# A written instruction order for the first tiles and weight units of a hybrid encoder step

## The chip, the cores and the metric

The kernel runs on one core of one Trainium2 chip. The metric is the device time of one execution in microseconds (us): before the change 1288.83 us, the median of three runs from 1287.74 to 1289.24.

## The reference

Two layers act on 640 token rows (512 of a prompt, 8 groups of 16 of a sample), each 1024 channels wide. Layer 0 is a chunked gMLP, layer 1 an attention with a forgetting bias. The change touches only the start of layer 0:

```python
hp = rms_norm(xp, norm_pre[i])                     # x * rsqrt(mean(x*x) + 1e-6) * g
proj = h @ w_in                                    # (rows, 1024) @ (1024, 6144)
uv = jax.nn.gelu(proj[..., :2 * E])                # E = 2048: u, then v; z is the last third
v = layer_norm(uv[..., E:], ln_g, ln_b)            # v = the second third of proj
```

What follows (the mask over chunks, the product with the gate, the attention, the output projections, the per-layer embedding) is the same code on both sides.

## The kernel before, in words

The 640 rows are five tiles of 128 (t = 0 to 4; four of the prompt, one of the sample). The third of the projection that gives v is computed first, in four panels p of 512 columns. For one panel the product runs over the 1024 channels in eight blocks of 128 (k = 0 to 7); five accumulators, one per tile, stand in five banks of the accumulation memory (pb, eight banks).

Products are made precise by splitting: each operand becomes a high part, rounded to a short format by ScalarE (ACT, line 289), and a low part, the rest, by VectorE (DVE, line 290). One product is then three matmuls on TensorE (PE): high by high, high by low, low by high (lines 272, 273, 274, in the function `mm3`). So one panel has 5 x 8 x 3 = 120 matmuls of 128x512.

Weights come in units of 512 KB, two channel blocks each (unit u has blocks 2u and 2u+1), through three buffers (RAW) into five places for split units (W). SyncE (SP) issues their loads from one list; a load into a RAW buffer waits until the split of the unit before in that buffer is done. `prefetch` splits units as far ahead as W has room, `weights(1)` hands out the next one.

A tile of x (two loads of 256 KB) is brought into the product's form in this chain: squares and their sum (the left half on ACT, line 423, the right on DVE, 424); the two sums added (427); mean and eps (301); the power -1/2 on GpSimd (POOL, 303); x scaled by it and by the gain, half by half (DVE, 431; the gain is broadcast over partitions by a matmul with ones into banks 3 and 4, line 410, and read from there); each half transposed in four 128x128 blocks on PE (317) into one of the banks 5, 6, 7; and split into high and low (289, 290) into A, whose first 4 channel blocks come from the left half.

Before the products there are matmuls on zeros: three at the start (401) and four (N_FILL) between tile 0's two transposed halves (417).

A scheduler that works with its own model of times puts the instructions of each engine in an order. The program text sets it only where it says so: `tc.issue_after(x)` (in the helper `queued`) keeps an instruction behind x on its engine. Before the change this is used at the start for the filling matmuls, for tile 1's squares and for the first weight split.

Of the kernel before, what the change touches and what calls it, by code (L numbers as in the profile page):

```python
# [19 lines left out]
AF = mybir.ActivationFunctionType  # L20
# [37 lines left out]
def hybrid_trunk(tc, x_prompt, x_sample, ck, cv, clf, p_prompt, p_sample, norm_pre, norm_post,  # L58
# [34 lines left out]
    def f(ap):  # L93
        return ap.bitcast(F32)
# [201 lines left out]
    def rstd_of(ss, eps, mean=False, keep=False):  # L296
        t = small()
        if mean:
            nc.vector.tensor_scalar(out=t, in0=ss, scalar1=eps, scalar2=None, op0=ALU.add)
        else:  # L300
            nc.vector.tensor_scalar(out=t, in0=ss, scalar1=1.0 / D, scalar2=eps, op0=ALU.mult, op1=ALU.add)  # L301
        q = small(keep=keep)
        behind["pool"] = nc.gpsimd.tensor_tensor(out=q, in0=t, in1=mhalf, op=ALU.pow)  # L303
        return q
# [79 lines left out]
    def r2(o, n, p=P):  # L384
        return R2[:p, o:o + n]
# [5 lines left out]
    warm = r2(8320, 512)  # L391
    nc.gpsimd.memset(grow, 0.0)
    nc.vector.memset(warm, 0.0)
    nc.vector.memset(ones, 1.0)
# [4 lines left out]

    for i in range(N_WARM):  # L400
        nc.tensor.matmul(PB[7][:, :256], warm[:, :P], warm[:, 256:], start=True, stop=True)
    fetch(1)
    for t in range(1, NT):
        for h in range(2):
            x_dma(nc.sync, t, h)
        fetch(t // 2 + 1)
    dma(CST[:, P:], consts[:, P:])
    gb = PB[3], PB[4]
    for h in range(2):
        nc.tensor.matmul(gb[h], ones, grow[:, h * 512:(h + 1) * 512], start=True, stop=True)  # L410

    def first_tile(c, hi, bv):
        if c == 0:
            behind["act"] = hi
            for i in range(N_FILL):
                with queued("pe"):
                    behind["pe"] = nc.tensor.matmul(PB[2][:, :256], warm[:, :P], warm[:, 256:], start=True, stop=True)

    for t in range(NT):
        x, xn = r2(t * D, D), r2(5120 + (t % 2) * D, D)  # L420
        ss = [small(), small()]
        with queued(*["act", "dve"] * (t == 1)):
            nc.scalar.activation(out=xn[:, :512], in_=x[:, :512], func=AF.Square, accum_out=ss[0])
            nc.vector.scalar_tensor_tensor(out=xn[:, 512:], in0=x[:, 512:], scalar=1.0, in1=x[:, 512:], op0=ALU.mult, op1=ALU.mult,
                                           accum_out=ss[1])
        sq = small()
        nc.vector.tensor_tensor(out=sq, in0=ss[0], in1=ss[1], op=ALU.add)
        rs = rstd_of(sq, RMS_EPS)
        for h in range(2):
            hs = slice(h * 512, (h + 1) * 512)  # L430
            behind["dve"] = nc.vector.scalar_tensor_tensor(out=xn[:, hs], in0=x[:, hs], scalar=rs, in1=gb[h], op0=ALU.mult, op1=ALU.mult)
        transposed_split(xn, lambda c: h_hi[:, 4 * c:4 * c + 4, t * P:(t + 1) * P],
                         lambda c: h_lo[:, 4 * c:4 * c + 4, t * P:(t + 1) * P], (5, 6, 7), first_tile if t == 0 else None)
        with queued(*["dve"] * (t == 0)):
            prefetch(t + 1)


    o_X, o_ln, o_sum, o_th = 14208, 15232, 16256, 17216
    HT = TOK // 2
# [828 lines left out]
```

## Time and profile before

| | |
|---|---|
| median of three runs | 1288.83 us |
| the profiled execution | 1288.87 us, of it span 1287.1 us |
| PE busy | 1271.9 us, 99% of the span |
| DVE, ACT, POOL busy | 962.9, 592.3, 356.6 us |
| granted PE clock over the span | 0.999 |
| first product of panel 0 starts | 11.18 us after the span's start |

The times of the profile are counted from the start of the span. PE is busy nearly throughout; matmuls overlap, so the length of one row is more than what it costs when others follow it, and the step from one start to the next is the price. The prediction shows the rows it uses.

### The profile page before, as it was taken

To read this page: it belongs to the slowest core of one execution; us is meant where nothing else is said; L and a number is where in the kernel's file an instruction comes from. 1 tells how busy PE (TensorE), PEld (TensorE's weight loads), DVE (VectorE), ACT (ScalarE), POOL (GpSimd) and SP (SyncE) were. 2 spreads that over 40 slices of the span, in tenths; PEclk is the share of its full clock that TensorE was granted. 3 is DMA by queue.
4 is the path that set the end of the run, shared out by engine and by line. 5 is a ranking of instruction groups with operands and counts; after the bars stand their busy time and mean duration, and the time that the engine had idled before them with its cause. 6 is when DMAs were issued, how large, how long until landed. Compare 5 with 4: busy or idle time off the path is not lost.

```text
span 1287.1 us, 21134 instructions
## 1 busy us (share of the span) xinstructions
PE 1271.9 (99%) x7881; PEld 1140.2 (89%) x7881; DVE 962.9 (75%) x1805; ACT 592.3 (46%) x1071; POOL 356.6 (28%) x328
## 2 busy tenths in 40 slices
PE   8999999999999999998999999999999999999998
PEld 6888999999988888887899999998999999788887
DVE  6744999999943364797987898989898988645643
ACT  4423554544545253563445454545444444545331
POOL 1012445454000010245344444444344430000100
PEclk9999999999999999999999999999999999999999
DMA  6432343323324212647787867677788748732211
GB/s 232 131 99 82 100 126 108 111 79 103 117 88 162 84 42 95 149 99 155 159 171 164 189 158 168 145 173 163 146 158 190 177 104 257 257 127 82 66 66 49
DMA packets 275264, 171.52 MB, mean 133 GB/s; under 512 B 188761, under 2 KB 238473, under 8 KB 275162
## 3 DMA queue, kind: packets, MB, share of 16 engines
q1 hardware_dynamic: 261170, 127.80, 36.2%
q0 software_dynamic: 10080, 36.89, 14.0%
q10 hardware_dynamic: 3912, 5.50, 1.3%
q8 instruction: 62, 1.02, 0.3%
q14 instruction: 40, 0.33, 0.1%
HBM read 148.55 MB, written 21.59 MB: 132 GB/s over the span
## 4 chain that ended last, share of the span: by engine, by line
PE 94%; DVE 3%; DMA 2%; issue 0%; ACT 0%; SPq 0%; POOL 0%; DVEq 0%; ACTq 0%; POOLq 0%
PE pb L272 27%; PE pb L273 27%; PE pb L274 27%; PE pb L1055 3%; PE pb L1132 1%; PE pb L1048 1%; PE pb L317 1%; PE pb L1105 1%; PE pb L621 1%; DVE W L290 1%; PE pb L920 1%; DMA R<-in_cache_fox_k 1%; PE pb L933 1%; DMA RAW<-in_gmlp_w_in 1%; PE pb L1129 1%; DMA r2a_t<-in_x_prompt 0%
## 5 line engine op out<-in xcount | busy, mean ns | idle before, releaser
L272 PE MATMUL pb<-A,W 128*128 128x320 f32 (+1 forms) x752 | 240.8, 320 | 2.9 <-DVE R L600 2.5
L273 PE MATMUL pb<-A,W 128*128 128x320 f32 (+1 forms) x752 | 233.7, 311 | 0.0
L274 PE MATMUL pb<-A,W 128*128 128x320 f32 (+1 forms) x752 | 233.2, 310 | 0.0
L290 DVE TENSOR_TENSOR W<-RAW,W 128x1024 fp32r<-128x1024 f32 (+1 forms) x126 | 152.9, 1214 | 74.7 <-ACT W L289 72.5
L272 PE MATMUL pb<-W,A 128*128 128x512 f32 x520 | 204.2, 394 | 0.6 <-ACT A L289 0.5
L273 PE MATMUL pb<-W,A 128*128 128x512 f32 x520 | 203.2, 391 | 0.6 <-DVE W L290 0.5
L274 PE MATMUL pb<-W,A 128*128 128x512 f32 x520 | 202.5, 392 | 0.0
L289 ACT ACTIVATE W<-RAW 128x1024 fp32r<-128x1024 f32 (+1 forms) x126 | 120.0, 953 | 95.2 <-PE pb L274 47.7
L272 PEld LDWEIGHTS pb<-A,W 128*128 128x128 f32 x752 | 141.7, 188 | 4.0 <-DVE R L600 2.7
L273 PEld LDWEIGHTS pb<-A,W 128*128 128x128 f32 x752 | 141.6, 188 | 0.6 <-issue 0.2
L274 PEld LDWEIGHTS pb<-A,W 128*128 128x128 f32 x752 | 141.2, 188 | 0.0
L303 POOL TENSOR_TENSOR SML<-SML 128x1 f32<-128x1 f32 x25 | 19.2, 771 | 372.6 <-DVE SML L301 367.9
L272 PE MATMUL pb<-tbf,W 128*128 128x320 f32 x360 | 119.0, 330 | 0.0
L273 PEld LDWEIGHTS pb<-W,A 128*128 128x128 f32 x520 | 97.7, 188 | 20.8 <-DVE W L290 1.4
L272 PEld LDWEIGHTS pb<-W,A 128*128 128x128 f32 x520 | 97.7, 188 | 20.5 <-ACT A L289 1.1
L274 PEld LDWEIGHTS pb<-W,A 128*128 128x128 f32 x520 | 97.5, 188 | 20.6 <-DVE A L290 0.5
L274 PE MATMUL pb<-tbf,W 128*128 128x320 f32 x360 | 111.4, 309 | 0.0
L273 PE MATMUL pb<-tbf,W 128*128 128x320 f32 x360 | 111.2, 309 | 0.0
L211 POOL TENSOR_TENSOR sff<-RAW 128x512 f32<-128x512 f32 x46 | 59.2, 1289 | 172.6 <-DVE W L290 111.3
L589 DVE TENSOR_TENSOR R<-R,pb 128x320 f32<-128x320 f32 x184 | 86.2, 476 | 15.6 <-PE pb L274 14.6
L290 DVE TENSOR_TENSOR A<-R,A 128x640 fp32r<-128x640 f32 (+1 forms) x42 | 34.4, 853 | 57.4 <-ACT A L289 56.9
L272 PEld LDWEIGHTS pb<-tbf,W 128*128 128x128 f32 x360 | 67.7, 188 | 9.9 <-issue 6.2
(274 smaller groups left out, 2821.8 us busy)
## 6 DMA issues: line engine op xcount, KB each, us to landing
RAW<-in_fox_w_in POOLq DMA_DIRECT2D x46, 512.0 KB, 6.9
RAW<-in_gmlp_w_in SPq DMA_DIRECT2D x40, 512.0 KB
R<-in_cache_fox_k SPq DMA_DIRECT2D x128, 128.0 KB
R<-in_cache_fox_v SPq DMA_DIRECT2D x32, 512.0 KB
RAW<-in_gmlp_w_out SPq DMA_DIRECT2D x16, 512.0 KB
RAW<-in_ple_w_gate SPq DMA_DIRECT2D x16, 512.0 KB
RAW<-in_fox_w_out SPq DMA_DIRECT2D x16, 512.0 KB
R<-in_fox_w_in POOLq DMA_DIRECT2D x14, 512.0 KB, 7.9
```

What stands on the lines that cost most here:

```text
L211: nc.gpsimd.tensor_tensor(out=o, in0=a, in1=b, op=op)
L272: nc.tensor.matmul(out, lh, rh, start=start, stop=False)
L273: nc.tensor.matmul(out, lh, rl, start=False, stop=False)
L274: nc.tensor.matmul(out, ll, rh, start=False, stop=stop)
L289: first = nc.scalar.activation(out=hi, in_=src, func=AF.Copy)
L290: nc.vector.tensor_tensor(out=lo, in0=src, in1=f(hi), op=ALU.subtract)
L303: behind["pool"] = nc.gpsimd.tensor_tensor(out=q, in0=t, in1=mhalf, op=ALU.pow)
L317: behind["pe"] = nc.tensor.transpose(out=b[:, j * P:(j + 1) * P], in_=src[:, (4 * c + j) * P:(4 * c + j + 1) * P], identity=ident)
L589: behind["dve"] = nc.vector.tensor_tensor(out=into(i, j), in0=a, in1=b, op=ALU.add)
L621: nc.tensor.matmul(b0[:, t * P:(t + 1) * P], v_at(pnl, t)[:, c0:c0 + P], wm, start=True, stop=True)
L920: nc.tensor.matmul(b, hi, w, start=k == 0, stop=False)
L1055: nc.tensor.matmul(O[:, d], v[:, j, hh * P:(hh + 1) * P], pt[:, j * P:(j + 1) * P], start=(j == 0), stop=(j == i))
```

## The change

For the first part of panel 0 the scheduler no longer decides. A helper `then` ties each instruction on PE, ACT and DVE behind the one written before it for that engine, so the text from `squares(0)` to `low(4, 1)` is the order. In it:

- Channel blocks 0 to 3 of all five tiles come first, so the right halves of tiles 1 to 4 are transposed and split late. Tiles 0 and 1 are multiplied in turns, then 2, 3 and 4.
- Tile 1's left half is scaled and transposed ahead of the first product; tile 0's two transposed halves stand together, and the four filling matmuls behind them.
- Weight units 0 and 1 are split in halves of 512 columns, 2 and 3 whole, into fixed places.
- SP loads tile 1's x ahead of weight unit 0; units 1 and 2 keep their places.
- x is scaled in place. The squares carry the factor 1/1024, so that adding the two sums and eps is one DVE instruction; for tiles 3 and 4 the squares are one ACT instruction over the whole tile.
- From tile 1's products with block 4 on, the loops of before go on and the scheduler decides again.

```diff
-    fetch(1)
     for t in range(1, NT):
         for h in range(2):
             x_dma(nc.sync, t, h)
-        fetch(t // 2 + 1)
+        if t != 3:
+            fetch(state["raw"] + 1)
...
-    for t in range(NT):
-        x, xn = r2(t * D, D), r2(5120 + (t % 2) * D, D)
...
-        transposed_split(xn, lambda c: h_hi[:, 4 * c:4 * c + 4, t * P:(t + 1) * P],
-                         lambda c: h_lo[:, 4 * c:4 * c + 4, t * P:(t + 1) * P], (5, 6, 7), first_tile if t == 0 else None)
-        with queued(*["dve"] * (t == 0)):
-            prefetch(t + 1)
+    def then(e, make, *args, **kw):
+
+        with ExitStack() as stack:
+            if e in line:
+                stack.enter_context(tc.issue_after(line[e].ins))
+            line[e] = make(*args, **kw)
...
+    def squares(t):
+
+        m, q, s = small(), small(), [small(), small()]
+        if t < 3:
+            then("act", act, out=junk[:, :512], in_=x_of(t, 0), func=AF.Square, scale=D ** -0.5, accum_out=s[0])
+            then("dve", mul, out=junk[:, 512:], in0=x_of(t, 1), scalar=1.0 / D, in1=x_of(t, 1), op0=ALU.mult, op1=ALU.mult, accum_out=s[1])
+            then("dve", mul, out=m, in0=s[0], scalar=RMS_EPS, in1=s[1], op0=ALU.add, op1=ALU.add)
+        else:
+            then("act", act, out=junk, in_=x_of(t), func=AF.Square, scale=D ** -0.5, accum_out=s[0])
+            then("dve", nc.vector.tensor_scalar, out=m, in0=s[0], scalar1=RMS_EPS, scalar2=None, op0=ALU.add)
+        nc.gpsimd.tensor_tensor(out=q, in0=m, in1=mhalf, op=ALU.pow)
+        factor[t] = q
...
+    squares(0)
+    scaled_by(0, 0)
+    scaled_by(0, 1)
+    turn_x(0, 0)
+    turn_x(0, 1)
+    for i in range(N_FILL):
+        then("pe", nc.tensor.matmul, PB[2][:, :256], warm[:, :P], warm[:, 256:], start=True, stop=True)
+    squares(1)
+    high(0, 0)
+    high(0, 1)
+    low(0, 0)
+    scaled_by(1, 0)
+    turn_x(1, 0)
+    w_high(0, 0)
+    w_high(0, 1)
+    w_low(0, 0)
+    w_low(0, 1)
+    high(1, 0)
+    low(1, 0)
+    products("hh00", "lh00", "hh01", "hl00", "lh01", "hh10", "hh11", "hl10", "hl01", "hl11", "lh10", "lh11")
+    squares(2)
+    w_high(1, 0)
...
+    products("hh02", "hh12", "lh02", "lh12", "hh03", "hh13", "lh03", "lh13")
+    turn_x(2, 0)
+    products("hl02", "hl12", "hl03", "hl13")
...
-        out = [bank((0, 1, 2, 3, 4, 5, 6, 7)) for _ in range(NT)]
+        out = v_out if p == 0 else [bank((0, 1, 2, 3, 4, 5, 6, 7)) for _ in range(NT)]
         for kk in range(4):
-            (w,) = weights(1)
-            for t in range(NT):
+            with queued(*["act", "dve"] * (p == kk == 0)):
+                (w,) = weights(1)
+            for t in range(kk == 2, NT) if p == 0 and kk >= 2 else range(NT if p else 0):
```

In a name such as `hl13` the letters are the part of x and the part of the weight (x high, weight low), the digits tile 1 and channel block 3. The new instructions are recorded at line 419, inside `then`.

How PE's list starts before the change, from the broadcast of the gain (into pb3 and pb4) to the first transposes of tile 1. pb5, pb6 and pb7 take transposes, pb0 to pb4 the products of tiles 0 to 4, pb2 the filling:

```order
L410 MATMUL pb4_74<-r2a_t_87 128x512
L317 MATMUL pb5_75<-CST_67,r2a_t_87 128x128 x4
L417 MATMUL pb2_72<-r2a_t_87 128x256 x4
L317 MATMUL pb6_76<-CST_67,r2a_t_87 128x128 x4
L272 MATMUL pb0_70<-W_63,A_65 128x512
L273 MATMUL pb0_70<-W_63,A_65 128x512
L274 MATMUL pb0_70<-W_63,A_65 128x512
```

and after it, the same place:

```order
L410 MATMUL pb4_74<-r2a_t_87 128x512
L419 MATMUL pb5_75<-CST_67,r2a_t_87 128x128 x4
L419 MATMUL pb6_76<-CST_67,r2a_t_87 128x128 x4
L419 MATMUL pb2_72<-r2a_t_87 128x256 x4
L419 MATMUL pb7_77<-CST_67,r2a_t_87 128x128 x4
L419 MATMUL pb0_70<-W_63,A_65 128x512 x5
L419 MATMUL pb1_71<-W_63,A_65 128x512 x3
L419 MATMUL pb0_70<-W_63,A_65 128x512
```

The filling moved behind tile 0's second block of transposes, tile 1's first block came ahead of all products, and products of tile 1 (pb1) now stand between those of tile 0. Before, twelve products of tile 0 stood here in a row, and tile 1's two blocks behind them.

DVE's list in the same stretch, from the scaling of tile 0 on (r2a_t is x, SML the small sums, A the split x, W the split weights). Before:

```order
L431 SCALAR_TENSOR_TENSOR r2a_t_87<-r2a_t_87,SML_68,pb4_74 128x512
L290 TENSOR_TENSOR W_63<-RAW_66,W_63 128x1024
L424 SCALAR_TENSOR_TENSOR r2a_t_87,SML_68<-r2a_t_87 128x512
L290 TENSOR_TENSOR A_65<-pb5_75,A_65 128x4x128
L427 TENSOR_TENSOR SML_68<-SML_68 128x1
L424 SCALAR_TENSOR_TENSOR r2a_t_87,SML_68<-r2a_t_87 128x512
L301 TENSOR_SCALAR SML_68<-SML_68 128x1
L290 TENSOR_TENSOR W_63<-RAW_66,W_63 128x1024
L290 TENSOR_TENSOR A_65<-pb6_76,A_65 128x4x128
```

and after:

```order
L419 SCALAR_TENSOR_TENSOR r2a_t_87<-r2a_t_87,SML_68,pb4_74 128x512
L419 SCALAR_TENSOR_TENSOR r2a_t_87,SML_68<-r2a_t_87 128x512
L419 SCALAR_TENSOR_TENSOR SML_68<-SML_68 128x1
L419 TENSOR_TENSOR A_65<-pb5_75,A_65 128x4x128
L419 SCALAR_TENSOR_TENSOR r2a_t_87<-r2a_t_87,SML_68,pb3_73 128x512
L419 TENSOR_TENSOR W_63<-RAW_66,W_63 128x512 x2
L419 TENSOR_TENSOR A_65<-pb7_77,A_65 128x4x128
```

Tile 1's square, its small sum and its scaling came ahead of the first weight split, which is now two halves; the low part of tile 0's right half (pb6) is no longer here.

More of the change, by code (lines that the diff above doesn't have):

```diff
@@ L390, in hybrid_trunk @@
     grow, ones = r2(7168, D), r2(8192, P)
-    warm = r2(8320, 512)
+    warm, junk = r2(8320, 512), r2(5120, D)
     nc.gpsimd.memset(grow, 0.0)
@@ L410, in hybrid_trunk @@
         nc.tensor.matmul(gb[h], ones, grow[:, h * 512:(h + 1) * 512], start=True, stop=True)
[L412 to L417, printed above, removed]
-    for t in range(NT):
-        x, xn = r2(t * D, D), r2(5120 + (t % 2) * D, D)
[L421 to L431, printed above, removed]
-        transposed_split(xn, lambda c: h_hi[:, 4 * c:4 * c + 4, t * P:(t + 1) * P],
-                         lambda c: h_lo[:, 4 * c:4 * c + 4, t * P:(t + 1) * P], (5, 6, 7), first_tile if t == 0 else None)
-        with queued(*["dve"] * (t == 0)):
-            prefetch(t + 1)
@@ new lines, in hybrid_trunk, with x_of @@
+    line = {}
+    def then(e, make, *args, **kw):
[3 more added lines that the diff above has]
+            line[e] = make(*args, **kw)
+    act, add, mul = nc.scalar.activation, nc.vector.tensor_tensor, nc.vector.scalar_tensor_tensor
+    factor, turned = {}, {}
+    def x_of(t, h=None):
+        return r2(t * D, D) if h is None else r2(t * D + h * 512, 512)
+    def squares(t):
[9 more added lines that the diff above has]
+        factor[t] = q
@@ new lines, in scaled_by, with turn_x, part @@
+    def scaled_by(t, h):
+        then("dve", mul, out=x_of(t, h), in0=x_of(t, h), scalar=factor[t], in1=gb[h], op0=ALU.mult, op1=ALU.mult)
+    def turn_x(t, c):
+        b = bank((5, 6, 7))
+        for j in range(4):
+            then("pe", nc.tensor.transpose, out=b[:, j * P:(j + 1) * P], in_=x_of(t, c)[:, j * P:(j + 1) * P], identity=ident)
+        turned[t, c] = b.rearrange("p (k n) -> p k n", k=4)
+    def part(z, t, c):
+        return (h_hi, h_lo)[z][:, 4 * c:4 * c + 4, t * P:(t + 1) * P]
@@ new lines, in high, with low, w_high, w_low @@
+    def high(t, c):
+        then("act", act, out=part(0, t, c), in_=turned[t, c], func=AF.Copy)
+    def low(t, c):
+        then("dve", add, out=part(1, t, c), in0=turned[t, c], in1=f(part(0, t, c)), op=ALU.subtract)
+    def w_high(u, z, n=512):
+        o = u * 2048 + z * 512
+        then("act", act, out=W[:, o:o + n], in_=raw_of(u)[:, z * 512:z * 512 + n], func=AF.Copy)
+    def w_low(u, z, n=512):
+        o = u * 2048 + z * 512
+        then("dve", add, out=W[:, o + 1024:o + 1024 + n], in0=raw_of(u)[:, z * 512:z * 512 + n], in1=f(W[:, o:o + n]), op=ALU.subtract)
@@ new lines, in hybrid_trunk, with product, products, four @@
+    v_out = [bank() for _ in range(NT)]
+    begun = set()
+    def product(form, t, k):
+        o = (k // 2) * 2048 + (k % 2) * 512
+        lhs, rhs = h_at(k, t * P, (t + 1) * P)[form == "lh"], W[:, o + 1024 * (form == "hl"):][:, :512]
+        then("pe", nc.tensor.matmul, v_out[t], lhs, rhs, start=t not in begun, stop=(form, k) == ("lh", 7))
+        begun.add(t)
+    def products(*which):
+        for x in which:
+            product(x[:2], int(x[2]), int(x[3]))
+    def four(t):
+        return [g + str(t) + str(k) for g in ("hh", "hl", "lh") for k in range(4)]
@@ new lines, in hybrid_trunk @@
+    squares(2)
+    w_high(1, 0)
+    w_high(1, 1)
+    w_low(1, 0)
+    scaled_by(2, 0)
+    w_low(1, 1)
+    squares(3)
+    products("hh02", "hh12", "lh02", "lh12", "hh03", "hh13", "lh03", "lh13")
+    turn_x(2, 0)
+    products("hl02", "hl12", "hl03", "hl13")
+    high(2, 0)
+    low(0, 1)
+    low(2, 0)
+    scaled_by(3, 0)
+    squares(4)
+    scaled_by(1, 1)
+    products(*four(2)[:6])
+    turn_x(3, 0)
+    products(*four(2)[6:])
+    high(3, 0)
+    scaled_by(4, 0)
+    low(3, 0)
+    scaled_by(4, 1)
@@ new lines, in hybrid_trunk @@
+    scaled_by(2, 1)
+    scaled_by(3, 1)
+    products(*four(3)[:2])
+    turn_x(4, 0)
+    high(4, 0)
+    low(4, 0)
+    products(*four(3)[2:])
+    turn_x(1, 1)
+    w_high(2, 0, 1024)
+    high(1, 1)
+    low(1, 1)
+    w_low(2, 0, 1024)
+    products(*four(4)[:6])
+    turn_x(2, 1)
+    high(2, 1)
+    low(2, 1)
+    products(*four(4)[6:])
+    turn_x(3, 1)
+    high(3, 1)
+    low(3, 1)
+    fetch(4)
+    w_high(3, 0, 1024)
+    w_low(3, 0, 1024)
+    products(*[g + "0" + k for k in "45" for g in ("hh", "hl", "lh")])
@@ L438, in hybrid_trunk @@
+    turn_x(4, 1)
+    high(4, 1)
+    low(4, 1)
+    for u in range(4):
+        place.append(range(2 * u, 2 * u + 2))
+        last_use[2 * u:2 * u + 2] = [u] * 2
+    behind.update(act=line["act"], dve=line["dve"])
     o_X, o_ln, o_sum, o_th = 14208, 15232, 16256, 17216
```

## The prediction

> **What bounds the kernel now.** I read the page first, then the busy time by stretches, then the timeline of the first 26 us.
>
> ```profile
> span 1287.1 us, 21134 instructions
> PE 1271.9 (99%) x7881; PEld 1140.2 (89%) x7881; DVE 962.9 (75%) x1805; ACT 592.3 (46%) x1071; POOL 356.6 (28%) x328
> ...
> PE 94%; DVE 3%; DMA 2%; issue 0%; ACT 0%; SPq 0%; POOL 0%; DVEq 0%; ACTq 0%; POOLq 0%
> ```
>
> TensorE (PE) is the bound: 94% of the chain that ended last. Only its idle time can be won. The stretches (columns: us, then PE, weight loads, DVE, ACT, POOL busy) say where that idle time is:
>
> ```profile
> 0.00:22.00 22.00, 18.74 (x68) 11.74 (x69) 14.90 (x31) 12.30 (x22) 3.81 (x8) 1.00 0.81 290
> 22.00:60.00 38.00, 38.00 (x177) 31.57 (x176) 28.26 (x36) 15.37 (x19) 1.09 (x2) 1.00 0.34 104
> 60.00:120.00 60.00, 60.00 (x266) 49.29 (x265) 27.79 (x27) 17.32 (x25) 9.56 (x9) 1.00 0.32 93
> ```
>
> From 22 us on PE never stops for 100 us. The instruction lists of all five engines join again near PE's 190th instruction, inside panel 1, apart from a swap or two of neighbours. So the change is worth what it wins or loses before PE is fed for good, and the rest should shift by that amount. PE's own rows around the head:
>
> ```profile
> 11.18 0.47 PE L272 MATMUL pb<-W,A 128*128 128x512 f32 x1
> ...
> 12.95 0.40 PE L272 MATMUL pb<-W,A 128*128 128x512 f32 x1
> 13.88 0.50 PE L273 MATMUL pb<-W,A 128*128 128x512 f32 x1 [0.53 <-DVE W L290]
> ...
> 15.20 1.31 PE L317 MATMUL pb<-CST,r2a_t 128*128 128x128 f32 x8
> 16.66 0.99 PE L272 MATMUL pb<-W,A 128*128 128x512 f32 x2
> ...
> 19.54 0.48 PE L272 MATMUL pb<-W,A 128*128 128x512 f32 x1
> 20.48 0.50 PE L272 MATMUL pb<-W,A 128*128 128x512 f32 x1 [0.45 <-ACT A L289]
> ...
> 21.95 0.40 PE L273 MATMUL pb<-W,A 128*128 128x512 f32 x1
> 22.19 0.39 PE L274 MATMUL pb<-W,A 128*128 128x512 f32 x1
> ...
> 25.60 0.39 PE L274 MATMUL pb<-W,A 128*128 128x512 f32 x1
> ```
>
> Matmuls overlap, so I count from start to start, not by durations. From 22.19 to 25.60 lie 15 products: 3.41/15 = 0.227 us each when nothing waits. Four transposes ("a block") cost, in the chain of waits:
>
> ```profile
> 19.35 0.45 PE pb L317 x4
> ...
> 21.21 0.44 PE pb L317 x4
> ```
>
> that is 0.445. Between the first product at 11.18 and the 26th at 21.95 PE had 25 products and 4 blocks: 25 x 0.227 + 4 x 0.445 = 7.46 of 10.77 us. **3.31 us are stall**, among it at 12.95, at 15.2 to 16.7 and at 19.5: each time PE had used up tile 0 and waited for a split of a weight unit or of x.
>
> **The yardstick.** Panel 0 needs 120 products either way. Ahead of a PE that runs without pause, before spends 11.18 (first product) + 3.31 (stall) + 8 blocks after the first product x 0.445 = 18.05 us. After the change tile 1's first block stands ahead of the first product, so 7 blocks = 3.12 are left. Gain = 18.05 - 3.12 - first product - new stalls = **14.93 - first product - new stalls**. The first product may come 2 us later than 11.18 and the change still wins: what counts is that it then does not stop.
>
> **When the first product comes.** It now stands behind tile 0's two blocks, the four filling matmuls and tile 1's first block, which needs x of tile 1 scaled. DVE's and POOL's prices:
>
> ```profile
> 4.98 3.75 PE L410 MATMUL pb<-r2a_t 128*128 128x512 f32 x4 [0.56 <-DMA r2a_t<-in_norm_pre]
> ...
> 5.25 0.16 DVE L427 TENSOR_TENSOR SML<-SML 128x1 f32<-128x1 f32 x1 [0.24 <-ACT r2a_t L423]
> 5.45 0.15 DVE L301 TENSOR_SCALAR SML<-SML 128x1 f32<-128x1 f32 x1
> 5.68 0.56 POOL L303 TENSOR_TENSOR SML<-SML 128x1 f32<-128x1 f32 x1 [4.00 <-DVE SML L301]
> ...
> 7.14 0.75 DVE L431 SCALAR_TENSOR_TENSOR r2a_t<-r2a_t,SML,pb 128x512 f32<-128x512 f32 x1 [1.54 <-PE pb L410]
> ...
> 7.94 0.18 PEld L317 LDWEIGHTS pb<-CST,r2a_t 128*128 128x128 f32 x1 [0.79 <-DVE r2a_t L431]
> 8.52 0.73 PE L317 MATMUL pb<-CST,r2a_t 128*128 128x128 f32 x4
> ...
> 8.77 0.75 DVE L431 SCALAR_TENSOR_TENSOR r2a_t<-r2a_t,SML,pb 128x512 f32<-128x512 f32 x1 [0.88 <-PE pb L410]
> ...
> 9.09 1.89 PE L417 MATMUL pb<-r2a_t 128*128 128x256 f32 x8
> ...
> 9.43 1.22 DVE L290 TENSOR_TENSOR W<-RAW,W 128x1024 fp32r<-128x1024 f32 x1
> ...
> 10.57 0.68 DVE L424 SCALAR_TENSOR_TENSOR r2a_t<-r2a_t 128x512 f32<-128x512 f32 x1
> ...
> 11.18 0.08 DVE L424 DVE_READ_ACCUMULATOR r2a_t<-r2a_t 128x1 f32 x1
> ```
>
> Merging the sum and the eps step (two small DVE instructions into one) gains nothing for tile 0: its first scaling at 7.14 waits for PE's broadcast of the gain (L410), as the row says, and its second, 8.77, too. Both stay. Then, on DVE: tile 1's square at 9.43 (where the weight split stood), its sum read out by 10.12 (0.61 + 0.08, as 10.57 to 11.26); the merged small instruction to about 10.30; POOL's power starts 0.08 later (5.60 to 5.68) and takes 0.56: 10.94; meanwhile tile 0's low part (0.68, in a row of 24.52 below) runs to 10.98; tile 1 scaled from 10.98; its block 0.80 later (7.14 to 7.94): 11.78. PE gets there in time: tile 0's second block at 8.77 + 0.80 = 9.57, then eight filling records:
>
> ```profile
> L417 PE MATMUL pb<-r2a_t x8: 379/379/382, 9.1 to 10.6; 128*128 128x256 f32 x8
> L401 PE MATMUL pb<-r2a_t x6: 634/634/797, 1.5 to 3.8; 128*128 128x256 f32 x6
> ```
>
> (from 9.1 to 10.6 seven steps: 0.215 each), so 9.57 + 0.43 + 8 x 0.215 = 11.72. **First product: 11.78 + 0.445 = 12.2.**
>
> **Do the products then run through?** In the new order, each against what it needs, with half-width splits at most the 0.68 (DVE) and 0.62 (ACT) of the 128x512 rows:
> - Weight unit 0 now loads behind tile 1's x. Two loads of x, one unit lie between these two ACT rows, so 512 KB take (11.50 - 7.48)/3 = 1.34 us, and the unit lands at 8.8. ACT wants it at 10.8, after tile 0's second high part: hidden by 2 us. Unit 1 and 2 keep their places in SP's list.
>
> ```profile
> 7.48 1.06 ACT L289 ACTIVATE W<-RAW 128x1024 fp32r<-128x1024 f32 x1 [2.26 <-DMA RAW<-in_gmlp_w_in]
> ...
> 11.50 1.06 ACT L289 ACTIVATE W<-RAW 128x1024 fp32r<-128x1024 f32 x1 [0.40 <-DMA RAW<-in_gmlp_w_in]
> ```
>
> - The 4th product (first with a low weight) starts at 12.9; DVE is done with that half at 10.98 + 0.70 + 0.69 = 12.4. Spare 0.5.
> - The 11th (tile 1's low part) starts at 14.5; DVE gets there by 13.7. Spare 0.8.
> - Tile 2's block, after 20 products, at 12.2 + 4.54 = 16.8. DVE from 13.7: square and small instruction to 14.6, half a weight split to 15.3, scaling, + 0.80. If POOL's power is held behind that split (next rows) it ends at 15.7 and the block could start at 16.55. Spare 0.2.
> - Tile 3's block, 0.445 + 10 products later, at 19.5; before it DVE takes tile 2's low part, for which ACT's high part ends at 18.0: 18.7, plus 0.80 = 19.5. **Spare 0.**
> - After that every block of DVE work (0.7) faces 6 products and a block of PE work (1.8), and the spare grows. The banks that hold the broadcast gain (pb3, pb4) are written by tiles 3's and 4's products; DVE has read them for the last time four and eight instructions after 18.7 (21.0 and 23.7), and those products stand at 21.3 and 24.9. The squares of tiles 3 and 4 move whole to ACT, which is busy 15.37 of 38 us between 22 and 60 and 12.30 of the 22 before; DVE loses two instructions of 0.68.
>
> New stalls: nothing if all goes so, some 0.4 at the zero-spare place if DVE slips; I take 0.15. **Sum: 14.93 - 12.2 - 0.15 = 2.6 us.** The profiled execution took 1288.87 us (1.77 around its span), 0.04 from the median of the runs, 1288.83; so 1286.3. Bounds for the first product: 11.72 + 0.445 (the filling sets it) to 12.6 (two more hand-overs of 0.2, as from 5.25 to 5.45), and 0 to 0.4 of stalls: gain 2.8 to 1.9.
>
> **POOL's power** can be slower than 0.56:
>
> ```profile
> 12.60 1.23 DVE L290 TENSOR_TENSOR W<-RAW,W 128x1024 fp32r<-128x1024 f32 x1
> ...
> 12.68 1.55 POOL L303 TENSOR_TENSOR SML<-SML 128x1 f32<-128x1 f32 x1 [6.45 <-DVE SML L301]
> ...
> 24.52 0.68 DVE L290 TENSOR_TENSOR A<-pb,A 128x512 fp32r<-128x512 f32 x1
> ...
> 24.68 0.55 POOL L303 TENSOR_TENSOR SML<-SML 128x1 f32<-128x1 f32 x1 [8.19 <-DVE SML L301]
> ```
>
> Beside a weight split (both inputs in SBUF) it took 1.55, until 0.4 after the split's end; beside a split of x (one input in PSUM) 0.55. In the new order tile 1's power runs beside a split of x, so I take 0.56. [...]
>
> **Rivals.**
> 1. *PE's clock opens later* (12%). The column of the granted clock reads 1.00 in every stretch, but the two rows of 128x256 matmuls above have the same form and take 634 and 379 ns, and a step is twice as long in the first: PE starts at half rate. It got full rate within tile 0's first block (8.52 to 9.09), 4.1 us after it began to work without pause at 4.98. Before, the filling follows at once; now PE pauses from 9.0 to 9.57. If the rate was not granted by then and the count begins again, full rate comes at 13.7: a block at 0.57, eight filling records at 0.427, the next block at 13.55, first product at 14.0, gain 0.9: 1288.0. For it: PE worked from 1.5 on, paused 0.56 us ahead of L410, and was not at full rate at 5. Against it: PE's work up to 9.09 is the same as before, and pauses once the rate was there (12.95 to 13.88) did no harm. [...]
> 2. *The same, one period longer* (7%): **slower**. If full rate takes two periods after 9.57 (17.8), the block runs at half rate too, first product 14.1, and 8 products until 17.8 take 0.454 instead of 0.227: +1.8. 14.93 - 14.1 - 1.8 = -1.0: 1289.9. It decides from the point where half rate lasts beyond about 15.8 (0.8 left after 14.1, at 0.227 lost per 0.454).
> 3. *POOL's power of tile 1 is held for 1.55* (6%): first product 13.2, gain 1.7: 1287.2. Against it: the 24.68 row.
> 4. *The gain is given back* (5%): PE reaches panel 1 earlier and waits there for weight splits: 1288.9. Against it: DVE is busy 28.26 of 38 us between 22 and 60, and units 0 and 1 now free their places in W at 28 us, when tile 4's products with them end, so later splits can start earlier.
>
> **How the numbers follow.** Forecast 70%: 1286.3, its own range 1285.6 to 1287.1 (bounds above, and some 0.3 of the 1.5 us by which the runs of before differ). With rivals 1 and 3 inside, 8 in 10 lie within 1285.4 to 1288.4. A change under 0.2% (2.6 us) is about what cannot be told from none: the forecast sits on that bound, so half of its 70% is "faster" (0.35); rivals 1, 3, 4 and the other half are "same"; of rival 2 about half is beyond 2.6 us with the spread of the runs (0.04 slower).
>
> **What would show it.** In the new profile: tile 1's first block near 11.8, first product near 12.2, the next 19 products at 0.227 each, no gap over 0.3 us up to 45 us; the same rows from panel 1 on about 2.6 us earlier. Filling records at 634 instead of 379 ns would be rivals 1 or 2; a power of 1.5 us before 12 us rival 3; PE waits for W after 40 us rival 4. The forecast is wrong if the first product comes after 13 us or PE stops for more than 0.5 us between 12 and 30 us.

## The result and the profile after

The changed kernel took **1285.82 us** (median of 14 runs, 1283.82 to 1286.84), against 1288.19 us (14 runs, 1286.79 to 1289.79) for the kernel before, timed beside it. The ratio is **0.9977, 95% interval 0.9969 to 0.9985**: faster by 0.23%, which is 1.9 to 4.0 us (the medians alone differ by 2.37 us). The time lies in the predicted range and the gain is near the predicted 2.6 us, but the interval is clear of "no change", to which most of the chance, 0.61, had been given.

The page of the profile after, its execution 1285.73 us:

```profile
span 1283.8 us, 21126 instructions
PE 1270.6 (99%) x7881; PEld 1141.6 (89%) x7881; DVE 961.3 (75%) x1798; ACT 593.3 (46%) x1073; POOL 357.0 (28%) x328
```

PE has the same 7881 instructions and 1.3 us less busy time; the rest of the 3.3 us of span is idle time that is gone. The busy time by stretches (us, then PE, weight loads, DVE, ACT, POOL) shows where:

```profile
0.00:22.00 22.00, 19.79 (x82) 14.26 (x83) 14.95 (x32) 10.52 (x21) 4.33 (x10) 1.00 0.77 266
22.00:60.00 38.00, 38.00 (x177) 31.46 (x176) 30.13 (x30) 19.04 (x23) 0.00 (x0) 1.00 0.46 147
60.00:120.00 60.00, 60.00 (x266) 49.28 (x265) 26.18 (x26) 17.93 (x26) 11.42 (x10) 1.00 0.28 81
```

In the first 22 us PE now starts 82 instructions instead of 68. Behind that it never stops, as before. The work of its neighbours grew between 22 and 60 us (DVE 28.26 to 30.13, ACT 15.37 to 19.04), and PE does not feel it.

PE's timeline of the head (start, duration, line, form, count, idle time ahead and who ended it). All of the new order is recorded at line 419; the first row is the broadcast of the gain, the rows of 128x128 are blocks of transposes, the last row is the 141st product, in panel 1:

```profile
4.73 3.29 PE L410 MATMUL pb<-r2a_t 128*128 128x512 f32 x4 [0.32 <-DMA r2a_t<-in_norm_pre]
7.86 0.60 PE L419 MATMUL pb<-CST,r2a_t 128*128 128x128 f32 x4
8.87 0.66 PE L419 MATMUL pb<-CST,r2a_t 128*128 128x128 f32 x4 [0.41 <-DVE r2a_t L419]
9.36 1.89 PE L419 MATMUL pb<-r2a_t 128*128 128x256 f32 x8
11.16 0.66 PE L419 MATMUL pb<-CST,r2a_t 128*128 128x128 f32 x4
11.57 4.83 PE L419 MATMUL pb<-W,A 128*128 128x512 f32 x20
16.24 0.60 PE L419 MATMUL pb<-CST,r2a_t 128*128 128x128 f32 x4
16.59 2.61 PE L419 MATMUL pb<-W,A 128*128 128x512 f32 x10
19.04 0.60 PE L419 MATMUL pb<-CST,r2a_t 128*128 128x128 f32 x4
...
46.80 0.39 PE L274 MATMUL pb<-W,A 128*128 128x512 f32 x1
```

Twenty products stand in one row without a wait, then ten; no later block of transposes waits for its x. In the kernel before, the same 141st product is the second matmul of this row, at 49.64 + 0.23 = 49.87:

```profile
49.64 0.62 PE L274 MATMUL pb<-W,A 128*128 128x512 f32 x2
```

So the head gained **3.07 us**, and the end of the program came 3.24 us earlier. This compares one execution of each kernel, and in the one of after the broadcast ended 0.71 us sooner (8.02 against 8.73). Counted from there the 141st product comes 2.36 us sooner; how much of the 0.71 the kernel before would have gained from a quicker broadcast too, no profile shows. By the prediction's yardstick: the first product is at 11.57; from it to the 141st pass 35.23 us, of which 140 products at 0.227 and 7 blocks at 0.445 are 34.90; new stalls are thus 0.33, and 14.93 - 11.57 - 0.33 = 3.03. The yardstick holds, its two terms moved. DVE's and POOL's timelines say why:

```profile
8.06 0.75 DVE L419 SCALAR_TENSOR_TENSOR r2a_t<-r2a_t,SML,pb 128x512 f32<-128x512 f32 x1 [0.43 <-PE pb L410]
8.73 0.68 DVE L419 SCALAR_TENSOR_TENSOR r2a_t<-r2a_t 128x512 f32<-128x512 f32 x1
...
10.36 0.75 DVE L419 SCALAR_TENSOR_TENSOR r2a_t<-r2a_t,SML,pb 128x512 f32<-128x512 f32 x1
...
13.99 0.69 DVE L419 TENSOR_TENSOR W<-RAW,W 128x512 fp32r<-128x512 f32 x1
```

```profile
9.77 0.55 POOL L437 TENSOR_TENSOR SML<-SML 128x1 f32<-128x1 f32 x1 [3.97 <-DVE SML L419]
14.13 0.96 POOL L437 TENSOR_TENSOR SML<-SML 128x1 f32<-128x1 f32 x1 [3.80 <-DVE SML L419]
```

Tile 0's second scaling started at 8.06 and not at 8.77, because the broadcast took 3.29 us and not 3.75, and began 0.25 us earlier. From it to the first product pass 3.51 us, 3.45 in the prediction.

### The profile page after: what moved, and what is told of

Same layout as the page of the kernel before. It is cut to its first block, busy times and chain, and to the rows that moved or that the text cites. A ratio compares the mean times of both kernels' runs of the same rounds, so it can differ in the third digit from the quotient of the medians.

```text
span 1283.8 us, 21126 instructions
## 1 busy us (share of the span) xinstructions
PE 1270.6 (99%) x7881; PEld 1141.6 (89%) x7881; DVE 961.3 (75%) x1798; ACT 593.3 (46%) x1073; POOL 357.0 (28%) x328
## 3 DMA queue, kind: packets, MB, share of 16 engines
q8 instruction: 62, 1.02, 0.3%
## 4 chain that ended last, share of the span: by engine, by line
PE 94%; DVE 3%; DMA 1%; issue 1%; SPq 0%; ACT 0%; POOL 0%; ACTq 0%; DVEq 0%; POOLq 0%
PE pb L272 26%; PE pb L274 26%; PE pb L273 26%; PE pb L1175 3%; PE pb L419 2%; PE pb L1252 1%; PE pb L1168 1%; PE pb L1225 1%; PE pb L741 1%; PE pb L317 1%; PE pb L1040 1%; DVE W L290 1%; DMA R<-in_cache_fox_k 1%; PE pb L1053 1%; DMA out<-R 1%
## 5 line engine op out<-in xcount | busy, mean ns | idle before, releaser
L290 DVE TENSOR_TENSOR W<-RAW,W 128x1024 fp32r<-128x1024 f32 (+1 forms) x122 | 147.4, 1209 | 72.6 <-ACT W L289 70.6
L273 PE MATMUL pb<-W,A 128*128 128x512 f32 x498 | 194.6, 391 | 0.0
L272 PE MATMUL pb<-W,A 128*128 128x512 f32 x498 | 194.5, 393 | 0.0
L274 PE MATMUL pb<-W,A 128*128 128x512 f32 x498 | 193.7, 392 | 0.0
L289 ACT ACTIVATE W<-RAW 128x1024 fp32r<-128x1024 f32 (+1 forms) x122 | 115.8, 949 | 90.0 <-PE pb L274 43.2
L303 POOL TENSOR_TENSOR SML<-SML 128x1 f32<-128x1 f32 x20 | 15.5, 776 | 350.7 <-DVE SML L301 345.9
L274 PEld LDWEIGHTS pb<-W,A 128*128 128x128 f32 x498 | 93.4, 188 | 19.4 <-issue 0.4
L273 PEld LDWEIGHTS pb<-W,A 128*128 128x128 f32 x498 | 93.6, 188 | 18.8
L272 PEld LDWEIGHTS pb<-W,A 128*128 128x128 f32 x498 | 93.5, 188 | 18.6
```

The lines of the kernel that those rows point to most:

```text
L272: nc.tensor.matmul(out, lh, rh, start=start, stop=False)
L273: nc.tensor.matmul(out, lh, rl, start=False, stop=False)
L274: nc.tensor.matmul(out, ll, rh, start=False, stop=stop)
L289: first = nc.scalar.activation(out=hi, in_=src, func=AF.Copy)
L290: nc.vector.tensor_tensor(out=lo, in0=src, in1=f(hi), op=ALU.subtract)
```

## The experiments

Each kernel was timed in five rounds beside the kernel before (median 1288.22 to 1288.32 in these series). Single executions of one kernel differ by 3 us, so two things are read: the ratio with its interval, and in the profile the starts of the first and of the 141st product, which do not depend on what happens later in the program. They do depend on the broadcast of the gain, which took from 1.94 to 3.75 us in these profiles, so the table has its end as well. "After" is the changed kernel.

| kernel | median us | ratio (95%) | broadcast ends | 2nd scaling of tile 0 | first product | 141st product |
|---|---|---|---|---|---|---|
| before (profile) |  |  | 8.73 | 8.77 | 11.18 | 49.87 |
| after | 1285.82 | 0.9977 (0.9969 to 0.9985) | 8.02 | 8.06 | 11.57 | 46.80 |
| after, a second time | 1285.64 | 0.9977 (0.9968 to 0.9986) | 7.79 | 7.82 | 11.33 | 46.53 |
| tile 0's products first | 1289.05 | 1.0006 (0.9997 to 1.0015) | 6.88 | 6.91 | 10.42 | 48.57 |
| filling 8 in after | 1287.20 | 0.9989 (0.9980 to 0.9998) | 6.85 | 6.89 | 12.00 | 47.20 |
| filling 8 in before | 1287.62 | 0.9994 (0.9985 to 1.0002) | 7.07 | 7.11 | 11.44 | 49.57 |
| no filling in after | 1286.46 | 0.9982 (0.9973 to 0.9991) | 7.39 | 7.43 | 10.94 | 46.16 |
| old load order in after | 1285.56 | 0.9979 (0.9970 to 0.9989) | 7.37 | 7.41 | 11.60 | 46.84 |
| new load order in before | 1288.67 | 1.0003 (0.9994 to 1.0012) | 8.01 | 8.05 | 11.36 | 50.79 |
| whole weight splits | 1284.33 | 0.9968 (0.9959 to 0.9978) | 8.06 | 8.10 | 11.60 | 47.15 |
| more work at the start | 1285.07 | 0.9979 (0.9970 to 0.9988) | 7.66 | 7.70 | 11.21 | 46.46 |
| right half off the way | 1284.64 | 0.9972 (0.9962 to 0.9983) | 6.98 | 8.91 | 10.88 | 46.19 |
| the same again | 1284.91 | 0.9973 (0.9962 to 0.9985) | 6.96 | 8.79 | 10.75 | 46.08 |
| the last two edits together | 1285.37 | 0.9979 (0.9970 to 0.9987) | 7.11 | 8.27 | 10.23 | 45.56 |

The theory under test is the prediction's: before, PE used up tile 0 and waited for splits; products of two tiles per weight unit remove these waits, and from tile 1's first block on PE itself is the bound. Rivals are that the new order of the loads, the halved splits or the place of the filling carry the gain.

### Tile 0's products first

Only PE's list is changed back towards the old order: tile 0's products stand in a row, tile 1's behind them, with the same loads, halves, filling and blocks.

```diff
-    products("hh00", "lh00", "hh01", "hl00", "lh01", "hh10", "hh11", "hl10", "hl01", "hl11", "lh10", "lh11")
+    products("hh00", "lh00", "hh01", "hl00", "lh01", "hl01")
...
-    products("hh02", "hh12", "lh02", "lh12", "hh03", "hh13", "lh03", "lh13")
+    products("hh02", "lh02", "hh03", "lh03", "hl02", "hl03", "hh10", "hh11", "hl10", "hl11", "lh10", "lh11", "hh12", "lh12", "hh13", "lh13")
     turn_x(2, 0)
-    products("hl02", "hl12", "hl03", "hl13")
+    products("hl12", "hl13")
```

> The changed kernel with one thing in PE's order undone: tile 0's products with channel blocks 0 to 3 all ahead of tile 1's, instead of the two tiles in turns; DVE, ACT and the loads as in the changed kernel. Theory A (tile 1's products are the work that covers the wait for weight unit 1): PE stops after tile 0's six products with unit 0, for unit 1's halves (ACT about 0.8 us, then DVE's second half about 1.6 us later in the list), 2 to 2.7 us of pauses before tile 2's block, and the gain over before falls to 0 to 0.7 us. Rival (having x of tile 1 and the splits early is enough, in whatever order PE takes them): gain stays above 2 us.

The ratio is 1.0006 (0.9997 to 1.0015): **the whole gain is gone**. PE's timeline of this kernel:

```profile
10.42 1.64 PE L419 MATMUL pb<-W,A 128*128 128x512 f32 x6
12.77 1.48 PE L419 MATMUL pb<-W,A 128*128 128x512 f32 x5 [0.71 <-ACT W L419]
15.38 2.80 PE L419 MATMUL pb<-W,A 128*128 128x512 f32 x11 [1.13 <-DVE SML L419]
...
48.57 0.39 PE L274 MATMUL pb<-W,A 128*128 128x512 f32 x1
```

Its first product is the earliest but one of all, 10.42, and it does not help: six products (1.36 us at 0.227 each) are all that unit 0 gives tile 0, PE is through at 11.8 and starts again at 12.77; five more, and the next pause ends at 15.38, with unit 1's second low half. DVE's timeline has that split behind tile 2's scaling:

```profile
14.64 0.68 DVE L419 TENSOR_TENSOR W<-RAW,W 128x512 fp32r<-128x512 f32 x1
```

From the first to the 141st product pass 38.15 us, 34.90 without stalls: 3.25 of stall, more than the expected 2 to 2.7 and as much as before (3.31 to the 26th product alone). The 141st product itself still comes 1.30 earlier than in the profile of before, because here the broadcast ended 1.85 earlier; this execution, 1287.14 us, was also the fastest of its eleven. Taking the turns of the two tiles away is enough to lose the gain. That the turns alone would bring it, without tile 1's early block and the late right halves, no run shows; nor was the merging of the small instructions or the move of squares to ACT taken back by itself.

### Twice the filling, in both kernels

```diff
-    N_WARM, N_FILL = 3, 4
+    N_WARM, N_FILL = 3, 8
```

> The changed kernel with eight filling matmuls instead of four behind tile 0's second block of transposes (1.7 us more of PE work ahead of tile 1's first block). Theory A (after the change PE alone sets the pace from tile 1's first block on, so a later first product is paid in full): the first product comes 1.7 us later after the start of tile 0's second scaling on DVE, products then run without pause, and the gain over the kernel before shrinks from about 2.5 to 0.8 to 1.1 us (part of the small stalls after it disappears). Theory B (DVE or ACT still set the pace, the gain is something else): no change, gain stays near 2.5 us.

> The kernel before with eight filling matmuls instead of four, ahead of tile 0's second block (1.7 us more of PE work). Theory A (before the change PE stood 3.3 us waiting for splits by DVE and ACT after its first product): the later first product is absorbed by those waits, time the same as before within 0.4 us, and the sum of PE's pauses up to 22 us falls by about 1.7 us. Theory B (before was bound by PE's start too): 1.7 us slower.

Eight further filling records are 8 x 0.215 = 1.7 us of work for PE that nobody needs. In the changed kernel (PE's timeline):

```profile
8.19 3.62 PE L419 MATMUL pb<-r2a_t 128*128 128x256 f32 x16
...
12.00 4.82 PE L419 MATMUL pb<-W,A 128*128 128x512 f32 x20
...
47.20 0.39 PE L274 MATMUL pb<-W,A 128*128 128x512 f32 x1
```

and in the kernel before:

```profile
7.63 3.62 PE L417 MATMUL pb<-r2a_t 128*128 128x256 f32 x16
...
11.44 0.48 PE L272 MATMUL pb<-W,A 128*128 128x512 f32 x1
...
16.96 0.99 PE L272 MATMUL pb<-W,A 128*128 128x512 f32 x2 [0.49 <-ACT W L289]
...
49.34 0.62 PE L274 MATMUL pb<-W,A 128*128 128x512 f32 x2
```

The kernel before takes the extra work for nothing: ratio 0.9994, its 141st product at 49.57 against 49.87. The changed one pays: the first product comes 5.11 us after the second scaling instead of 3.51, 1.6 later, and the ratio goes from 0.9977 to 0.9989, some 1.5 us. The intervals of these two ratios overlap a little, but the mean of its 11 runs, 1287.09 us, is 1.60 above that of the 24 runs of the change and its repeat, with a standard error of 0.32. Its 141st product is only 0.40 behind because the broadcast in this execution was quicker by 1.3 us. In the profile of the kernel before the broadcast was quicker too and ended 1.66 earlier, so the first product came only 0.26 later, and the pauses from it to the 141st product fell from 3.35 to 2.79 us, not by the expected 1.7; that this kernel hides the extra work is read from its time. So before, PE had room in the head; after, it has none.

### No filling

The same line with `N_FILL` at 0.

> The changed kernel without the four filling matmuls. Theory A (tile 1's scaling on DVE sets tile 1's first block, the filling only fits beside it, and PE's clock stays open once it was open): first product at the same place, time the same as the changed kernel within 0.4 us. Rival (the filling keeps the clock, or brings it): transposes or products at half rate for up to 4 us, 1 to 2 us slower than the changed kernel, gain over before 0.5 to 1.5 us.

```profile
7.45 1.44 PE L419 MATMUL pb<-CST,r2a_t 128*128 128x128 f32 x8
10.53 0.66 PE L419 MATMUL pb<-CST,r2a_t 128*128 128x128 f32 x4 [1.64 <-DVE r2a_t L419]
10.94 4.81 PE L419 MATMUL pb<-W,A 128*128 128x512 f32 x20
```

PE now stands still for 1.64 us ahead of tile 1's block, and the products behind that run at the same 4.81 for twenty as with filling (4.83). The first product is again 3.51 behind the second scaling: four fillings or none, tile 1's chain over DVE and POOL sets it. The ratio, 0.9982, is that of the change within its interval. In this execution a pause of this length, after full rate had come (the broadcast took 2.59 us, 3.75 in the profile of before), did not lower PE's rate.

### The order of the loads, each way

In the changed kernel the loop of before, and in the kernel before that of the change:

```diff
+    fetch(1)
     for t in range(1, NT):
         for h in range(2):
             x_dma(nc.sync, t, h)
-        if t != 3:
-            fetch(state["raw"] + 1)
+        fetch(t // 2 + 1)
```

> The changed kernel with the load order of the kernel before (weight unit 0 ahead of tile 1's x). Theory A (the written order of the products brings the gain; the loads have about the slack that the rows show): tile 1's x lands at about 8.8 us, just where DVE takes its square, so first product 0 to 0.4 us later and the gain over before still 2.0 to 2.5 us. Rival (the load order brings the gain): gain below 1 us.

> The kernel before with the new load order alone (tile 1's x ahead of weight unit 0); PE's and ACT's lists stay as they are, on DVE one square moves ahead of the first weight split. Theory A (the loads are not what PE waited for): the weight split starts at 8.8 instead of 7.5 on ACT, pauses of PE the same within 0.5 us, time 0 to 0.6 us slower or the same. Rival (the load order brings part of the gain by itself): 1 us faster or more.

Neither moves the time: 0.9979 for the change with the old loads, 1.0003 for the kernel before with the new ones. It is not nothing in the head, though. DVE's timeline of the change with the old loads:

```profile
8.76 0.69 DVE L419 SCALAR_TENSOR_TENSOR r2a_t<-r2a_t 128x512 f32<-128x512 f32 x1 [0.61 <-DMA r2a_t<-in_x_prompt]
```

Tile 1's square waits for its load until 8.76. In the profile of after it started at 8.73, held by tile 0's scaling; here that scaling came at 7.41, and the load took its place: the first product comes 4.20 behind the scaling instead of 3.51. So, by these two profiles, x of tile 1 ahead of the weights is worth some 0.7 us when the broadcast is quick (ended at 7.37), and nothing when it is slow (8.02). It does not always come early enough: with the new order too, tile 1's square waited for its load until 8.16 in the profile of filling 8. In the kernel before, the new loads do not help its head either. In PE's timeline of that kernel the first product waits for ACT's split of x, and the eighth still for DVE's weight split; in ACT's, the split of weight unit 0, ahead of that split of x, waits for its load until 9.77, where 8.8 was expected:

```profile
11.36 0.49 PE L272 MATMUL pb<-W,A 128*128 128x512 f32 x1 [0.68 <-ACT A L289]
...
14.83 0.49 PE L273 MATMUL pb<-W,A 128*128 128x512 f32 x1 [0.66 <-DVE W L290]
```

```profile
9.77 1.06 ACT L289 ACTIVATE W<-RAW 128x1024 fp32r<-128x1024 f32 x1 [4.65 <-DMA RAW<-in_gmlp_w_in]
```

Its 141st product is at 50.79, 0.9 behind that of before, where the first product had not waited. The time shows none of it, so the loads alone are neither the gain nor a loss that can be told.

### Whole weight splits

```diff
-    w_high(0, 0)
-    w_high(0, 1)
-    w_low(0, 0)
-    w_low(0, 1)
+    w_high(0, 0, 1024)
+    w_low(0, 0, 1024)
```

and so for unit 1, whose whole low part now stands ahead of tile 2's scaling.

> The changed kernel with weight units 0 and 1 split whole instead of in halves (the low part of unit 1 ahead of tile 2's scaling). Theory A (halves matter only through when DVE reaches what PE needs next): first low weight product just in time, tile 2's block about 0.4 us late, 0.3 to 0.7 us of pauses more than the changed kernel, gain over before still about 2 us. Rival (the halves are what lets PE start): first product over 1 us later, gain below 1.3 us.

PE's and POOL's timelines:

```profile
11.60 4.99 PE L419 MATMUL pb<-W,A 128*128 128x512 f32 x20
16.54 0.66 PE L419 MATMUL pb<-CST,r2a_t 128*128 128x128 f32 x4
```

```profile
14.16 1.55 POOL L437 TENSOR_TENSOR SML<-SML 128x1 f32<-128x1 f32 x1 [3.81 <-DVE SML L419]
```

The head does what the halves should prevent: POOL's power is held for 1.55 us, until 0.41 after the end of the whole low split (14.07 + 1.23 = 15.30), tile 2's block starts 4.94 behind the first product instead of 4.67, and the 141st product is 0.35 behind that of after. The time does not follow: 1284.33 us, ratio 0.9968, is the lowest of all, though its interval overlaps that of after. The profiled execution itself was the longest of its nine (1287.75 us), so its later part says nothing on that median. Halving the splits is thus not what carries the gain; why the whole ones were not slower by the 0.35 of the head stays open.

### Reaching the first product earlier

Two edits try to beat the change. The first gives PE more work at the start, on the author's theory that it is then at full rate sooner:

```diff
     for i in range(N_WARM):
         nc.tensor.matmul(PB[7][:, :256], warm[:, :P], warm[:, 256:], start=True, stop=True)
+    for i in range(3):
+        nc.tensor.matmul(PB[7][:, :64], warm[:, :P], warm[:, 256:320], start=True, stop=True)
```

> The changed kernel with three more small matmuls on zeros (64 columns, 0.21 us each) right behind the three at the start, so that PE has no pause of 0.5 us ahead of the broadcast of the gain. Theory (full rate comes one period after PE works without pause; the head of the changed kernel pays for a late first product in full): full rate during the broadcast or before it in most executions, tile 0's second scaling 1.8 to 2.6 us after the broadcast starts instead of 2 to 3.8, first product near 11 us, 0.4 to 0.8 us faster than the changed kernel, about 3.2 us faster than before. Rival (full rate comes at a moment that has nothing to do with PE's work ahead): same as the changed kernel.

```profile
5.38 2.28 PE L412 MATMUL pb<-r2a_t 128*128 128x512 f32 x4
```

The added matmuls ran from 4.21 to the broadcast, 1.17 us where 0.63 was expected, and into the time in which the gain had landed, so the broadcast began at 5.38, later than in any other run (4.71 to 5.17). Time and head are those of the change: from the end of the broadcast to the 141st product pass 38.80 us, in the profile of after 38.78. That more work at the start brings full rate sooner is not shown: the broadcast took 2.28 us here and 1.94 with both edits, and 1.95 to 3.29 in the other profiles of the written order.

The second takes tile 0's right half, which no early product needs, off the way of tile 1: scaling and transposes of the left half, two fillings (`N_FILL` at 2), then tile 1's square, and the right half beside tile 1's.

```diff
-    scaled_by(0, 1)
     turn_x(0, 0)
-    turn_x(0, 1)
...
     squares(1)
-    high(0, 0)
-    high(0, 1)
-    low(0, 0)
+    scaled_by(0, 1)
     scaled_by(1, 0)
+    turn_x(0, 1)
     turn_x(1, 0)
+    high(0, 0)
+    low(0, 0)
...
     products("hh00", ..., "lh11")
+    high(0, 1)
```

> The changed kernel with tile 0's right half taken off the way to the first product: on DVE tile 1's square and small sum come ahead of the scaling of tile 0's right half, which fills the wait for POOL's power; ACT's split of that half goes behind tile 1's; two filling matmuls instead of four. Theory A: tile 1's block about 1 us earlier, first product 0.8 to 1.1 us earlier after the start of the broadcast, but DVE's splits then have less time, so 0.3 to 0.5 us of pauses come back before tile 3's block: 0.4 to 0.7 us faster than the changed kernel. Rival (DVE is the bound by then, its work is the same): same as the changed kernel.

> The kernel with tile 0's right half off the way to the first product, once more, to compare it with the changed kernel in one series. Theory: 0.4 to 1.0 us faster than the changed kernel, so ratio to before about 0.0005 lower than that one's; not clear beyond the interval. Rival: the same ratio within 0.0003.

```profile
7.53 1.03 PE L419 MATMUL pb<-r2a_t 128*128 128x256 f32 x4
9.71 1.41 PE L419 MATMUL pb<-CST,r2a_t 128*128 128x128 f32 x8 [1.15 <-DVE r2a_t L419]
10.88 4.94 PE L419 MATMUL pb<-W,A 128*128 128x512 f32 x20
...
46.19 0.39 PE L274 MATMUL pb<-W,A 128*128 128x512 f32 x1
```

The 141st product is at 46.19 and 46.08, against 46.80 and 46.53 for the change. But in both profiles the broadcast ended earlier, at 6.98 and 6.96; counted from there, 39.21 and 39.12 us pass, more than the 38.78 and 38.74 of the change. DVE's timeline of the first says why:

```profile
8.03 0.69 DVE L419 SCALAR_TENSOR_TENSOR r2a_t<-r2a_t 128x512 f32<-128x512 f32 x1 [1.05 <-DMA r2a_t<-in_x_prompt]
```

Tile 1's square, now free to start early, waits for its load. These two heads do not show a gain; with a later broadcast there might be one. The 14 runs of the two series have a mean of 1284.84 us, the 24 runs of the change and its repeat 1285.49: 0.65 us less, with standard errors of 0.27 and 0.20, so two standard errors of the difference (0.33) apart, at the edge of what can be told, and not from one series. The unchanged kernel run again beside the second of them:

> The changed kernel once more, beside the three others of this series and the same runs of the kernel before. Theory: ratio to before within 0.997 to 0.9985; in its profile the first product again 3.5 us after the start of tile 0's second scaling, whatever the time that the broadcast of the gain took (1.95 to 3.75 us so far), and 0.4 to 0.5 us of pauses after it. If the moment of full rate were not what moves the first product, its distance from the broadcast's start would be the same as in the first profile (6.8 us).

gave 0.9977 again, so the result itself repeats. The first product came 3.51 behind the second scaling and 6.52 behind the start of the broadcast, against 6.84 in the first profile, so it goes with the end of the broadcast, as expected. Both edits together:

> The edits of a_warm and a_late together. Theory: the first product comes earliest of all, near 10 us, but tile 1's x (lands at 7 to 7.5 us) and DVE's splits set the pace, so the sum of both gains is not reached: 0.6 to 1.2 us faster than the changed kernel, 3.2 to 3.8 us faster than before. Rival: no faster than the better of the two alone.

```profile
5.17 1.94 PE L412 MATMUL pb<-r2a_t 128*128 128x512 f32 x4
...
10.23 4.94 PE L421 MATMUL pb<-W,A 128*128 128x512 f32 x20
```

have the earliest head of all, 10.23 and 45.56, and a ratio of 0.9979, no better than the change. From the end of the broadcast this head is 0.33 shorter than that of after (38.45 against 38.78). No version here is clearly faster than the change: a gain of the head below 1 us is lost in the spread of the runs.

## Why the prediction was right and where it was wrong

- **PE is the bound, and only its idle time in the head can be won; the rest shifts.** Right in these two profiles: 3.07 us at the 141st product, 3.24 at the end, PE 38.00 of 38.00 busy in the stretch behind. Over all fourteen profiles the time from the 141st product to the end of the span differs by 2.6 us, from 1236.1 to 1238.7, so one pair of them could not have shown it alone.
- **The yardstick, 14.93 - first product - new stalls.** Right in form: it gives 3.03 for the profile after, 3.07 measured. Its claim that a later first product costs nothing if PE then does not stop is shown from both sides: 11.57 instead of 11.18 and faster; 10.42 with tile 0 first, and not faster.
- **First product at 12.2.** Mis-sized, it was 11.57 and in the repeat 11.33. The chain from tile 0's second scaling was right within 0.06 (3.51 for 3.45, in the six profiles with this chain), and so was the order of its links: tile 1's DVE work and POOL, not the filling, which no filling at all confirms. What was off is its start: the prediction took the second scaling's 8.77 from the one profiled execution of before. That execution had the slowest broadcast of the fourteen profiled, 3.75 us; in the profiles of after and of its repeat the second scaling came at 8.06 and 7.82.
- **New stalls 0.15.** It was 0.33. Tile 2's block found its x ready (spare 0.2 predicted), and tile 3's, with "spare 0", too; the stall is spread in pieces below 0.2.
- **Weight unit 0 behind tile 1's x, landed at 8.8 and hidden by 2 us.** Right that it is hidden, wrong by how much. In after ACT took it at 10.06 without a wait; but with the same load order it was waited for until 9.77 in the kernel before, and in the changed kernel with tile 0's products first until 9.43. So by these two some 0.3 to 0.6 us were spare in after, and not 2. The loads alone move no time either way.
- **POOL's power 0.56 for tile 1; for tile 2, if held, until 0.4 after the split.** Right: 0.55 at 9.77; and 0.96 from 14.13 to 15.09, 0.41 after the split of 13.99 + 0.69 = 14.68. Rival 3 did not come.
- **Rivals 1 and 2, the clock.** Not seen. The pause was there (0.41 us ahead of the second block), and the filling behind it took 1.89 for eight, full rate, as in before; with 1.64 us of pause and no filling, the products ran at full rate too (4.81 for twenty). But what they need, a pause before full rate has come, did not occur: in after the last of the broadcast's four records took 0.60 us against 1.02 to 1.19 for the others, so the rate had come by 8.02, ahead of the pause, and in every profile of a kernel with the written order it came within the broadcast or before it (1.94 to 3.29 us for the four records; 3.75 in before, where the last was no faster than the two ahead of it). That a pause ahead of it would put full rate off by another 4.1 us, or by two such periods, was the author's estimate from one execution (4.98 to 9.09); no run shows it. The half-rate block of 0.57 in rival 1's sum was too short besides: it is a block of before in which the rate changed, its four records taking 0.41, 0.30, 0.27 and 0.27 us. Nothing hung on it.
- **Rival 4, given back at panel 1.** Not seen: no waits of PE behind 22 us that the stretches show.
- **The chances: the failed step.** "A change under 0.2% (2.6 us) is about what cannot be told from none: the forecast sits on that bound, so half of its 70% is 'faster'." With 0.35 the sign had less than even odds, although the argument left little room for a gain below 1.9 us. Two things were wrong in it. The first alone decides: the resolution was put at 0.2% without a measurement, and 14 runs of each kernel resolved 0.08%, so a gain of 2.6 us would have been told from none as well. The second is the size of the largest term: with the first product of after or of its repeat, 11.57 or 11.33, and 0.33 of stall the sum is 3.0 or 3.3 us and no longer on the bound. How much of this is the change and how much a luckier draw of the broadcast stays open: with the 8.77 of before and the measured 3.51 and 0.33 the same sum gives 2.3. The 23% that rivals 1, 3 and 4 added to "same" came on top.

## What to carry to other kernels

Where the bounding engine waits at the start for operands that are made one unit at a time, let each prepared unit feed two tiles before the next is needed; here nothing of the gain was left without that, while the loads and the size of the splits could be taken back and it stayed. Judge such a head by the start of a product well behind it and not by its first product: a first product at 10.42 here belonged to a kernel no faster than the one before. And a start time taken from one profile is one draw: count from the event that varies, here the end of the broadcast (6.85 to 8.73 us), and ask which waits of the old kernel absorb a late one, and whether the new kernel still has them.

## What the runs showed of the hardware that was not expected

**The same first matmuls take very different times.** The broadcast of the gain, four matmuls of 128x512, took from 1.94 us (both edits together, 5.17) over 3.29 (after) to 3.75 (before), and ended between 6.85 and 8.73 in the fourteen profiles. The profiles of before and of filling 8 in the changed kernel have the longest and nearly the shortest, with a pause ahead of it that is about as long (0.56 and 0.49 us). Its four records, from the view of line 410 (shortest/median/longest in ns, then the first and last start), before and in filling 8:

```profile
L410 PE MATMUL pb<-r2a_t x4: 1061/1061/1192, 5.0 to 7.7; 128*128 128x512 f32 x4
```

```profile
L410 PE MATMUL pb<-r2a_t x4: 592/592/667, 4.9 to 6.3; 128*128 128x512 f32 x4
```

Apart from the two kernels with more work at the start, the work up to there is the same and the broadcast starts between 4.71 and 4.98. The column of the granted clock reads 1.00 over the first 22 us in the four profiles that were read by stretches (before, after, its repeat, tile 0's products first), so no row names the cause. The records do show that PE's rate differs: from start to start they are some 0.9 us apart in the one and 0.45 in the other, and in after the last takes 0.60 us, the three ahead of it 1.02 to 1.19. So PE ran at the higher rate from 4.9 us on in one execution and not before 8.5 in another. The changed kernel passes an early end on to its first product (3.50 or 3.51 us behind the second scaling in six profiles). The kernel before seems to hide it in its waits, as it hides twice the filling; no profile of it with an early end and four fillings was taken. So the moment at which the rate rises differed by over 3 us between executions whose work up to there is the same; what sets it, no run shows.

**The granted clock of whole executions goes with their time, but loosely.** Of the change's 14 runs the two with a mean granted clock of 1.000 took 1283.9 us on average, the four at 0.997 1286.6, nearly all of the 3 us by which these runs differ and as much as the whole change is worth. The runs between do not line up (1285.2 at 0.998, 1285.5 at 0.999), and in the 87 runs of the kernel before that stood beside the experiments it is far less: 1288.5 for the 33 at 0.998, 1288.1 for the six at 1.000. What sets either is not shown.
